# Two-part activations in one pass, 48 gathered tokens, gate tiles on GpSimd, in a two-block transformer kernel

## The chip, the cores and the metric

One core of a Trainium2 chip runs the whole program. The metric is device time in microseconds (us) of one execution; the figures for the kernel before are the median and the spread of three runs. A profiled execution of the same kernel gives the trace.

## The reference, cut to what matters

Two transformer blocks of width 1024 run over 256 tokens. Each has a mixer (attention) and then a feed-forward layer that picks single-neuron experts. The change is in that feed-forward layer alone. In both blocks it is the following computation; the second block has its own weights and half as wide queries.

```
def peer_ffn_2(hn, w_peer_q, sub_keys1, sub_keys2, expert_u, expert_v):
    ...
    s1 = jnp.einsum('thd,hkd->thk', q[:, :, 0], sub_keys1)
    s2 = jnp.einsum('thd,hkd->thk', q[:, :, 1], sub_keys2)
    v1, i1 = lax.top_k(s1, PEER_TOPK)          # 16 of 128 keys, 8 heads
    v2, i2 = lax.top_k(s2, PEER_TOPK)
    ...
    sc, pos = lax.top_k(cand, PEER_TOPK)       # 16 of 256 sums
    eidx = jnp.take_along_axis(cidx, pos, axis=-1)   # expert 128 * i1 + i2
    gates = jax.nn.softmax(sc, axis=-1)
    ...
    act = jax.nn.gelu(jnp.einsum('nkd,nd->nk', expert_u[e], xt), approximate=False)
    return jnp.einsum('nk,nkd->nd', g * act, expert_v[e])
```

There are 16384 experts, so `expert_u` and `expert_v` are 64 MB each in fp32. Each token takes 8 x 16 = 128 of them.

## The kernel before, in words

**Two ways to the same sum.** The feed-forward layer is the method `peer` (L907). For 224 of the 256 tokens (`DENSE`) it is dense: all 16384 activations are computed, multiplied with a matrix of gates that is zero for experts not chosen, and summed with all of `expert_v`. For the last 32 tokens (`GATHERED`) the chosen rows of both tables are fetched by index. The 32 tokens times 128 experts lie as 128 partitions by 32 columns: partition p holds token p mod 32 and a quarter of its experts, so each column j is one indirect DMA of 128 rows of 4 KB from GpSimd's queue (`fetch`, L1201).

**Arithmetic in two parts.** An fp32 number is split into a high part in the format fp32r and a low part, the rest. A product is three matmuls: high by high, high by low, low by high (`mm3`, L350). The tokens are split once into `ht`, a tile with both parts next to each other. Weights stream: SyncE's queue loads units of 128 x 1024 fp32 (512 KB) into four `raw` buffers (L313), ScalarE copies the high part (`hi`, L325), VectorE subtracts to get the low part (`lo`, L334). The high and low tiles have three buffers each, and `unit` keeps two units of parts ahead of the matmuls, in program order.

**Order of the work.** Everything is written out in Python in one program order. After each unit of matmuls `tick` advances every running generator by one step, then runs pieces of the top-k up to a budget (`FILL_U`, 1.2 a tick), then issues the waiting `lo`. Each engine works through its own instructions in that order.

**Stage U.** 128 blocks of 128 experts. `project_t` (L497) makes the activations of one block: for each of eight chunks of the width, three matmuls of 224 columns through `mm3` (L353, L354, L355). Two blocks share a PSUM bank; then `activated` (L1047) applies GELU on ScalarE from PSUM into `ga` (128 x 128 x 224 in SBUF), or, for tokens whose gates are there already, GELU in place in PSUM and a VectorE product with `ga` (L1054). The first 40 or so blocks run beside the top-k, which is on VectorE. Then `group` (L1015) makes the gate matrix for four tokens at a time: two one-hot tiles per token by comparing an `iota` row with the token's index (`o2`, L1027, or on ScalarE at L1022 and L1023 for two of four; `o1`, L1028, times the gate), eight fp16 matmuls (L1034, L1035), and one step of ScalarE or VectorE that writes or multiplies `ga` (L1041, L1043). 56 groups are spread up to block 122.

**The gathered tokens.** `spread_picks` (L1167) copies indices, gates and norm factors of the 32 tokens to the 128 partitions with matmuls and small copies. `gathers` (L1186) then runs 64 jobs through three buffers `gathered`: 32 dot products of fetched rows with the token (VectorE, L1216, one every three ticks), and, once V has begun, 32 scaled sums of rows of the second table (VectorE, L1228, one every two ticks). After each job the next fetch goes to GpSimd's queue.

**Stage V.** 128 blocks again; the eight PSUM banks hold the sums of eight chunks of the width. `add_rows` (L1096) uses two matmuls: the high part of the weights by both token parts next to each other, 448 columns (L1099), and the low part by the high token part, 224 columns, into the second half (L1100). `weigh` (L1092) splits four blocks of `ga` at a time (ScalarE L346, VectorE L347). At the end of the layer the halves are added, turned back with transposes (L1141), the gathered sums are folded from 128 partitions to 32 tokens by a matmul (L1136), and both are added into x (`add_to_x`, L528).

Of the kernel before, what the change touches and what calls it, by code (L numbers as in the profile page):

```python
# [24 lines left out]
GATHERED = 32  # L25
DENSE = 256 - GATHERED
SHARE = 128 // GATHERED
# [9 lines left out]
def _columns():  # L37

    off, table = 0, {}
    for name, n in (("ident", 128), ("norm_mix", 8), ("norm_ffn", 8), ("norm_ple", 8), ("norm1", 8),  # L40
                    ("norm2", 8), ("norm_o", 8), ("b_gate", 2), ("na_q", 1), ("na_k", 1), ("dil_q", 64),
                    ("dil_k", 64), ("cos", 16), ("sin", 16), ("vmask", 8), ("kmask", 32), ("ends", 2), ("repeat", 128),
                    ("fold", GATHERED)):
# [52 lines left out]
def _arrays(a):  # L96
# [104 lines left out]
    put(cst, "repeat", p[:, None] == 128 - GATHERED + p[None, :] % GATHERED)  # L201
    put(cst, "fold", p[:, None] % GATHERED == np.arange(GATHERED)[None, :])
# [30 lines left out]
class Kernel:  # L233
# [269 lines left out]

    def begin_t(self, ht, outs):
# [402 lines left out]
    def peer(self, n, sides_apart, aim, prefetch):  # L907
# [107 lines left out]
        def group(g):  # L1015
            o2 = side.tile([128, 4, 128], F16, tag="o2", name="o2", bufs=2)
            o1 = work.tile([128, 4, 128], F32, tag="row4", name="o1", bufs=2)
            n = self.BY_SCALAR
            if n:
                away = side.tile([128, n, 128], F16, tag="away", name="away", bufs=1)  # L1020
                for j in range(n):
                    nc.scalar.activation(away[:, j], self.iota, AF.Abs, scale=-1.0, bias=i2t[:, 4 * g + j:4 * g + j + 1])  # L1022
                nc.scalar.activation(o2[:, :n], away, AF.Relu, scale=-1.0, bias=1.0)  # L1023
# [23 lines left out]
        def activated(pair, b):  # L1047
            s = slice(2 * pair, 2 * pair + 2)
            t0 = 4 * state["groups"]
            if t0 < DENSE:  # L1050
                self.curve(ga[:, s, t0:], b[:, :, t0:], AF.Gelu)
# [4 lines left out]
            return  # L1056
            yield
# [5 lines left out]
        for blk in range(128):  # L1063
            if blk % 2 == 0:
                b = self.bank().rearrange("p (j t) -> p j t", j=2)[:, :, dense]
            self.project_t(ht, b[:, blk % 2], dense)
            if blk % 2:
# [882 lines left out]
```

## Time and profile before

| | |
|---|---|
| median of three runs | 1943.38 us (1942.16 to 1945.08) |
| the profiled execution | 1939.94 us, span 1938.2 us |
| TensorE matmul busy | 1913.2 us (99%) |
| VectorE busy | 1551.3 us (80%) |
| ScalarE busy | 1131.0 us (58%) |
| GpSimd busy | 181.8 us (9%) |
| moved by DMA | 412.39 MB, mean 213 GB/s |
| first layer: U, then V from | 277.8 us, 654.0 us |
| second layer: U, then V from | 1218.5 us, 1598.3 us |

Engines are named PE (TensorE matmul), PEld (TensorE weight load), DVE (VectorE), ACT (ScalarE), POOL (GpSimd) and SP (SyncE). Times run from the start of the span. Matmuls overlap each other, so the spacing of their starts tells their cost, not their length; a VectorE row is some 0.08 us longer than its spacing too. Durations on POOL are rough.

### The profile page before, as it was taken

How to read it: one execution, taken by the hardware profiler on the slowest of the kernel's cores; microseconds unless marked ns; L12 is line 12 of the kernel's file. 1: busy time of each engine (PE TensorE's matmuls, PEld its weight loads, DVE VectorE, ACT ScalarE, POOL GpSimd, SP SyncE). 2: the span in 40 equal slices, each digit the busy share in tenths (PEclk: the TensorE clock that was granted, in tenths of full speed). 3: DMA queues.
4: the chain of work that ended last, by engine and by line, in shares of the span. 5: the costliest groups of instructions: out<-in, count | busy, mean ns of one | idle time of the engine just before them, and what ended most of it. 6: DMA issues, size and time to landing. Idle time of an engine off the chain costs nothing.

```text
span 1938.2 us, 37562 instructions
## 1 busy us (share of the span) xinstructions
PE 1913.2 (99%) x14666; PEld 1815.0 (94%) x14666; DVE 1551.3 (80%) x3188; ACT 1131.0 (58%) x1833; POOL 181.8 (9%) x142
## 2 busy tenths in 40 slices
PE   8999999999999999999999999999999999999997
PEld 7899999999999999999979979999999999999997
DVE  6865899989999877765577568998899997787655
ACT  5555555577776554445465655555777765545554
POOL 1000000010010223300000000000100012333000
PEclk9999999999999999999999999999999999999999
DMA  7453556667777888776654324566677778888663
GB/s 251 151 159 103 177 164 198 197 220 230 234 230 230 271 292 313 294 241 210 216 168 150 109 63 156 175 204 193 221 225 228 222 229 295 301 313 310 219 226 120
DMA packets 114433, 412.39 MB, mean 213 GB/s; under 512 B 12720, under 2 KB 13888, under 8 KB 114256
## 3 DMA queue, kind: packets, MB, share of 16 engines
q1 hardware_dynamic: 93168, 337.16, 54.1%
q0 software_dynamic: 18432, 67.12, 9.9%
q10 hardware_dynamic: 2656, 5.73, 0.9%
q8 instruction: 115, 1.88, 0.4%
q14 instruction: 62, 0.51, 0.1%
HBM read 408.90 MB, written 1.05 MB: 212 GB/s over the span
## 4 chain that ended last, share of the span: by engine, by line
PE 87%; DVE 9%; ACT 2%; issue 1%; DMA 1%; DVEq 0%; ACTq 0%
PE bank L1099 21%; PE bank L353 16%; PE bank L354 16%; PE bank L355 16%; PE bank L1100 10%; DVE lo L334 4%; DVE o L1028 1%; PE bank L1034 1%; PE bank L1035 1%; PE bank L1775 1%; DVE gathered L1216 1%; DVE ga L1043 1%; PE bank L512 1%; DVE repeated L1228 1%; ACT hi L325 0%
## 5 line engine op out<-in xcount | busy, mean ns | idle before, releaser
L325 ACT ACTIVATE hi<-raw 128x1024 fp32r<-128x1024 f32 x639 | 675.6, 1059 | 692.4 <-PE bank L354 288.0
L334 DVE TENSOR_TENSOR lo<-raw,hi 128x1024 fp32r<-128x1024 f32 x639 | 772.2, 1218 | 104.2 <-ACT hi L325 103.8
L353 PE MATMUL bank<-ht,hi 128*128 128x224 f32 (+1 forms) x2336 | 654.8, 280 | 0.0
L1099 PE MATMUL bank<-ht,hi 128*128 128x448 f32 x2048 | 650.1, 376 | 0.5 <-DVE ht L347 0.5
L355 PE MATMUL bank<-ht,lo 128*128 128x224 f32 (+1 forms) x2336 | 643.2, 275 | 1.2 <-DVE lo L334 1.2
L354 PE MATMUL bank<-ht,hi 128*128 128x224 f32 (+1 forms) x2336 | 642.8, 275 | 0.0
L1100 PE MATMUL bank<-ht,lo 128*128 128x224 f32 x2048 | 544.6, 266 | 1.6 <-DVE lo L334 0.3
L355 PEld LDWEIGHTS bank<-ht,lo 128*128 128x128 f32 x2336 | 447.5, 192 | 1.9 <-DVE lo L334 1.7
L353 PEld LDWEIGHTS bank<-ht,hi 128*128 128x128 f32 x2336 | 447.0, 191 | 1.7 <-ACT hi L325 0.3
L354 PEld LDWEIGHTS bank<-ht,hi 128*128 128x128 f32 x2336 | 447.4, 192 | 0.0
L1099 PEld LDWEIGHTS bank<-ht,hi 128*128 128x128 f32 x2048 | 384.1, 188 | 35.8 <-DVE ht L347 0.9
L1100 PEld LDWEIGHTS bank<-ht,lo 128*128 128x128 f32 x2048 | 391.1, 191 | 7.5 <-DVE lo L334 7.5
L1205 POOL DMA_INDIRECT gathered<-in_rows_dram,index x64 | 69.2, 1082 | 1224.2 <-DVE o L1028 440.6
L347 DVE TENSOR_TENSOR ht<-ga,ht 128x896 fp32r<-128x896 f32 (+2 forms) x78 | 75.6, 979 | 125.5 <-ACT ht L346 125.5
L1028 DVE TENSOR_SCALAR o<-iota,i1t,pack 128x128 f32<-128x128 f16 x448 | 142.6, 340 | 0.0
L1205 POOL DMA_INDIRECT gathered<-in_v_dram,index x64 | 105.0, 1640 | 227.5 <-DVE repeated L1228 191.3
L354 PE MATMUL bank<-lo,ht 128*128 128x512 f32 (+1 forms) x224 | 80.1, 358 | 2.7 <-DVE lo L334 2.7
L353 PE MATMUL bank<-hi,ht 128*128 128x512 f32 (+1 forms) x224 | 81.7, 365 | 0.5 <-ACT hi L325 0.5
L355 PE MATMUL bank<-hi,ht 128*128 128x512 f32 (+1 forms) x224 | 80.0, 357 | 0.6 <-DVE ht L447 0.6
L1228 DVE SCALAR_TENSOR_TENSOR repeated<-gathered,pick_dot,repeated 128x1024 f32<-128x1024 f32 x62 | 79.3, 1279 | 0.0
L1216 DVE CUSTOM_DVE_ANT_0 gathered<-gathered,repeated 128x1024 f32<-128x1024 f32 x64 | 77.7, 1215 | 0.0
L1022 ACT ACTIVATE away<-iota,i2t 128x128 f16<-128x128 f16 x224 | 76.3, 390 | 0.0
(363 smaller groups left out, 2129.8 us busy)
## 6 DMA issues: line engine op xcount, KB each, us to landing
raw<-in_u_dram SPq DMA_DIRECT2D x256, 512.0 KB, 4.2
raw<-in_v_dram SPq DMA_DIRECT2D x256, 512.0 KB, 4.7
raw<-in_w_qkv_dram SPq DMA_DIRECT2D x30, 512.0 KB, 4.3
raw<-in_w_q_dram SPq DMA_DIRECT2D x24, 512.0 KB, 3.5
raw<-in_w_t_dram SPq DMA_DIRECT2D x21, 512.0 KB, 3.6
raw<-in_w_gates_dram SPq DMA_DIRECT2D x16, 512.0 KB, 3.5
raw<-in_w_branch_dram SPq DMA_DIRECT2D x14, 512.0 KB, 3.5
raw<-in_w_pg_dram SPq DMA_DIRECT2D x8, 512.0 KB, 4.3
```

The costliest lines, as they stand in the source:

```text
L325: self.nc.scalar.activation(parts[0], raw, AF.Copy)
L334: self.nc.vector.tensor_tensor(lo, raw, hi.bitcast(F32), op=OP.subtract)
L353: mm(out, l[0], r[0], start=start, stop=False, **kw)
L354: mm(out, l[0], r[1], start=False, stop=False, **kw)
L355: mm(out, l[1], r[0], start=False, stop=stop, **kw)
L1022: nc.scalar.activation(away[:, j], self.iota, AF.Abs, scale=-1.0, bias=i2t[:, 4 * g + j:4 * g + j + 1])
L1028: nc.vector.tensor_scalar(o1[:, j], self.iota, i1t[:, t:t + 1], pf[:, t:t + 1], op0=OP.is_equal, op1=OP.mult)
L1099: mm(acc[c], v[0][:, c], weights[i][:, :, j], start=blk == 0, stop=False, skip_group_check=True)
L1100: mm(acc[c][:, 1], v[1][:, c], weights[i][:, 0, j], start=False, stop=blk == 127, skip_group_check=True)
L1205: nc.gpsimd.indirect_dma_start(out=rows[i], out_offset=None, in_=tables[t], in_offset=bass.IndirectOffsetOnAxis(ap=picks["index"][:, j:j + ...
L1216: nc.vector.tensor_tensor_reduce(r, r, picks["normed"], 1.0, 0.0, OP.mult, OP.add, w[:, j:j + 1])
L1228: nc.vector.scalar_tensor_tensor(total, r, w[:, j:j + 1], total, op0=OP.mult, op1=OP.add)
```

## The change

Five things change, in both layers.

1. U uses two matmuls per chunk as V does (`project_pairs`): the high weights by both token parts, and the low weights by the high part into the second half. A block now has its own PSUM bank; `activated` copies the second half to SBUF on ScalarE, adds the first half on VectorE into a tile `total`, and applies GELU and the gate product there. It runs over several ticks, and V begins only when it is done.
2. 48 tokens are gathered, in sets of 32 and 16 (`SETS`); `DENSE` is 208, and there are 52 groups. The set of 16 has eight partitions per token and 16 columns. There are 96 jobs instead of 64.
3. All gate tiles are made on GpSimd, two ticks ahead of their matmuls instead of one.
4. 14 dots are spread over the last 86 blocks of U; the other 34 and all 48 sums over the first 116 ticks of V. The sums of both sets are interleaved; those of the small set run on GpSimd as a scaling and an addition.
5. Spreading the picks uses a mask and a reduction; folding uses one more bank, two matmuls and one more addition.

The diff, cut (tables of constants and pool declarations left out):

```
-GATHERED = 32
-DENSE = 256 - GATHERED
+SETS = ((32, 96), (16, 80))
+DENSE = 256 - sum(n for n, _ in SETS)
+FOLD = 64
...
+    def project_pairs(self, ht, out, s):
+        w = self.unit(8)
+        mm = self.nc.tensor.matmul
+        for k in range(8):
+            pair = ht[k // 4][:, :, k % 4, s]
+            mm(out, w[0][:, k], pair, start=k == 0, stop=False, skip_group_check=True)
+            mm(out[:, 1], w[1][:, k], pair[:, 0], start=False, stop=k == 7, skip_group_check=True)
+        self.tick()
...
         def group(g):
-            n = self.BY_SCALAR
-            ...
             for j in range(4):
                 t = 4 * g + j
-                if j >= n:
-                    nc.vector.tensor_scalar(o2[:, j], self.iota, i2t[:, t:t + 1], None, op0=OP.is_equal)
-                nc.vector.tensor_scalar(o1[:, j], self.iota, i1t[:, t:t + 1], pf[:, t:t + 1],
+                nc.gpsimd.tensor_scalar(o2[:, j], self.iota, i2t[:, t:t + 1], None, op0=OP.is_equal)
+                nc.gpsimd.tensor_scalar(o1[:, j], self.iota, i1t[:, t:t + 1], pf[:, t:t + 1],
                                         op0=OP.is_equal, op1=OP.mult)
+            yield
             yield
...
-        def activated(pair, b):
+        def activated(pair, banks):
+            total = pool.tile([128, 2, DENSE], F32, tag="total", name="total", bufs=2)
+            yield
+            for j, b in enumerate(banks):
+                nc.scalar.activation(total[:, j], b[:, 1], AF.Copy)
+                nc.vector.tensor_tensor(total[:, j], b[:, 0], total[:, j], op=OP.add)
+                yield
             ...
-                self.curve(b[:, :, :t0], b[:, :, :t0], AF.Gelu)
-                nc.vector.tensor_tensor(ga[:, s, :t0], ga[:, s, :t0], b[:, :, :t0], op=OP.mult)
+                self.curve(total[:, :, :t0], total[:, :, :t0], AF.Gelu)
+                nc.vector.tensor_tensor(ga[:, s, :t0], ga[:, s, :t0], total[:, :, :t0], op=OP.mult)
...
-            self.project_t(ht, b[:, blk % 2], dense)
-            if blk % 2:
-                self.start(activated(blk // 2, b))
+            pair.append(self.bank()[:, :2 * DENSE].rearrange("p (s t) -> p s t", s=2))
+            if blk % 2 == 0:
+                self.start(activated(blk // 2, pair))
+            self.project_pairs(ht, pair[-1], dense)
...
-        while state["groups"] < n_groups:
+        while state["groups"] < n_groups or state["blocks"] < 128:
...
+            for j, name in enumerate(("index", "gate")):
+                part = t[:, j].rearrange("p (g m) -> p g m", m=m)
+                nc.vector.tensor_tensor(part, b[:, 128 * j:128 * (j + 1)].rearrange("p (g m) -> p g m", m=m), own, op=OP.mult)
+                nc.vector.tensor_reduce(t[:, 2 + j, :m], part.rearrange("p g m -> p m g"), AX.X, OP.add)
+                nc.vector.tensor_copy(p[name], t[:, 2 + j, :m])
...
-    EVERY = (3, 2)
+    DOTS, LAST_PICK = 14, 116
...
+        def job(at):
+            t, i, j = jobs[at]
+            r, p = rows.pop(at), picks[i]
+            w, total = p["dot"], p["rows"]
             if t == 0:
-                nc.vector.tensor_tensor_reduce(r, r, picks["normed"], 1.0, 0.0, OP.mult, OP.add, w[:, j:j + 1])
+                nc.vector.tensor_tensor_reduce(r, r, total, 1.0, 0.0, OP.mult, OP.add, w[:, j:j + 1])
+            elif j == 0:
+                nc.vector.tensor_scalar(total, r, w[:, :1], None, op0=OP.mult)
+            elif i == 0:
+                nc.vector.scalar_tensor_tensor(total, r, w[:, j:j + 1], total, op0=OP.mult, op1=OP.add)
             else:
+                nc.gpsimd.tensor_scalar(r, r, w[:, j:j + 1], None, op0=OP.mult)
+                nc.gpsimd.tensor_tensor(total, total, r, op=OP.add)
...
+        while at < len(jobs):
+            yield
+            if rate is None and "second" in self.done:
+                rate, due = (len(jobs) - at) / self.LAST_PICK, 0.0
+            due += rate or self.DOTS / 86
+            while due >= 1.0 and at < len(jobs):
+                due -= 1.0
+                ...
+                job(at)
+                fetch(at + 3)
+                at += 1
```

## Rows read from the trace of the kernel before

**Rows 1.** Busy time by window, with granted clock, DMA share and GB/s.
```profile
core 0: us, PE busy (x) PEld busy (x) DVE busy (x) ACT busy (x) POOL busy (x), PEclk, DMA share, GB/s
278.00:340.00 62.00, 62.00 (x558) 62.00 (x557) 61.93 (x269) 36.88 (x42) 0.00 (x0) 1.00 0.62 192
430.00:590.00 160.00, 160.00 (x1560) 159.13 (x1560) 152.39 (x370) 116.09 (x252) 16.96 (x18) 1.00 0.73 231
690.00:850.00 160.00, 158.83 (x979) 146.25 (x978) 124.82 (x109) 77.89 (x77) 46.97 (x28) 1.00 0.79 293
1650.00:1800.00 150.00, 150.00 (x949) 141.78 (x949) 119.39 (x104) 75.34 (x75) 45.97 (x28) 1.00 0.89 309
```

**Rows 2.** Timeline of PE in U: start us, length us, engine, line, operation.
```profile
603.02 0.28 PE L353 MATMUL bank<-ht,hi 128*128 128x224 f32 x1
...
603.36 0.27 PE L353 MATMUL bank<-ht,hi 128*128 128x224 f32 x1
...
603.70 0.23 PE L1034 MATMUL bank<-o,o 128*128 128x128 f16 x1
...
604.13 0.35 PE L353 MATMUL bank<-ht,hi 128*128 128x224 f32 x1
604.32 0.28 PE L354 MATMUL bank<-ht,hi 128*128 128x224 f32 x1
```

**Rows 3.** Timeline of PE in V, first and last of 16 pairs.
```profile
880.42 0.38 PE L1099 MATMUL bank<-ht,hi 128*128 128x448 f32 x1
...
885.48 0.38 PE L1099 MATMUL bank<-ht,hi 128*128 128x448 f32 x1
```

**Rows 4.** Timeline of DVE during the top-k, two neighbouring splits.
```profile
318.55 1.21 DVE L334 TENSOR_TENSOR lo<-raw,hi 128x1024 fp32r<-128x1024 f32 x1
...
321.11 1.20 DVE L334 TENSOR_TENSOR lo<-raw,hi 128x1024 fp32r<-128x1024 f32 x1
```

**Rows 5.** Groups of DVE instructions: 970 to 990 us, then 430 to 590.
```profile
L1131 DVE TENSOR_TENSOR ga<-bank,ga 128x224 f32<-128x224 f32 x8 | 2.8, 387 | 2.5 <-ACT ga L1130 2.5
...
L334 DVE TENSOR_TENSOR lo<-raw,hi 128x1024 fp32r<-128x1024 f32 x53 | 64.4, 1214 | 0.0
L1028 DVE TENSOR_SCALAR o<-iota,i1t,pack 128x128 f32<-128x128 f16 x146 | 46.9, 344 | 0.0
L1216 DVE CUSTOM_DVE_ANT_0 gathered<-gathered,repeated 128x1024 f32<-128x1024 f32 x18 | 21.9, 1216 | 0.0
L1027 DVE TENSOR_SCALAR o<-iota,i2t 128x128 f16<-128x128 f16 x73 | 18.9, 259 | 0.0
```

**Rows 6.** Timeline of PE: fp32 matmuls of 512 columns, repeating and folding.
```profile
398.15 1.02 PE L1193 MATMUL bank<-x,cst 128*128 128x512 f32 x2
...
981.92 1.04 PE L1136 MATMUL bank<-repeated,cst 128*32 128x512 f32 x2
```

**Rows 7.** Groups of POOL instructions other than DMA: busy us, mean ns.
```profile
L586 POOL MEMSET vdil<- 128x3072 f32 x1 | 2.6, 2648 | 0.0
...
L1735 POOL MEMSET attn<- 128x512 f32 x2 | 1.0, 524 | 0.0
L1887 POOL IOTA iota<- 128x256 f16 x1 | 0.4, 407 | 0.0
L589 POOL MEMSET weights<- 128x128 f32 x2 | 0.3, 194 | 0.0
L1889 POOL IOTA iota<- 128x128 f16 x1 | 0.2, 228 | 0.0
```

**Rows 8.** Timeline of POOL in U, and of DVE and POOL in V.
```profile
479.23 0.94 POOL L1205 DMA_INDIRECT gathered<-in_rows_dram,index  x1 [8.58 <-DVE o L1028]
...
722.67 2.35 DVE L334 TENSOR_TENSOR lo<-raw,hi 128x1024 fp32r<-128x1024 f32 x2
723.03 1.68 POOL L1205 DMA_INDIRECT gathered<-in_v_dram,index  x1 [5.31 <-DVE repeated L1228]
```

**Rows 9.** Groups of DVE instructions in V, 690 to 850 us.
```profile
L1228 DVE SCALAR_TENSOR_TENSOR repeated<-gathered,pick_dot,repeated 128x1024 f32<-128x1024 f32 x31 | 39.6, 1279 | 0.0
L347 DVE TENSOR_TENSOR ht<-ga,ht 128x896 fp32r<-128x896 f32 x16 | 17.5, 1092 | 33.1 <-ACT ht L346 33.1
```

**Rows 10.** DMA issues, median us to landing: 690 to 750, then 1700 to 1800.
```profile
gathered<-in_v_dram,index POOLq DMA_INDIRECT x12, 6.4
...
gathered<-in_v_dram,index POOLq DMA_INDIRECT x19, 8.2
```

More of the change, by code (lines that the diff above doesn't have):

```diff
@@ L530, in add_to_x @@
         end = at + src.shape[1]
-        xs = self.x[:, tt, at:end]
+        xs = self.x[:src.shape[0], tt, at:end]
         self.nc.vector.tensor_tensor(xs, xs, src, op=OP.add)
@@ L1135, in peer @@
                 s = slice(512 * half, 512 * (half + 1))
-                nc.tensor.matmul(banks[1][128 - GATHERED:, :], self.c("fold"), picks["sum"][:, s], start=True, stop=True)
+                folded = self.bank()
+                for i, p in enumerate(picks):
+                    nc.tensor.matmul(folded[FOLD:], self.c(f"fold{i}"), p["rows"][:, s], start=i == 0, stop=i == len(SETS) - 1)
                 for k in range(4):
@@ L1189, in gathers @@
             yield
-        for half in range(2):
-            s = slice(512 * half, 512 * (half + 1))
-            b = self.bank()
-            nc.tensor.matmul(b, self.c("repeat"), self.x[:, 1, s], start=True, stop=True)
-            yield
-            h = picks["normed"][:, s]
-            nc.vector.scalar_tensor_tensor(h, b, picks["y"][:, 1:2], h, op0=OP.mult, op1=OP.mult)
-        tables = (self.d[f"rows{n}"], self.d[f"v{n}"].rearrange("b p d -> (b p) d"))
-        jobs = [(t, j) for t in range(2) for j in range(GATHERED)]
@@ L1199, in gathers @@
-        rows = {}
-        def fetch(i):
-            if i < len(jobs):
-                t, j = jobs[i]
-                rows[i] = pool.tile([128, 1024], F32, tag="gathered", name="gathered", bufs=3)
-                nc.gpsimd.indirect_dma_start(out=rows[i], out_offset=None, in_=tables[t],
-                                             in_offset=bass.IndirectOffsetOnAxis(ap=picks["index"][:, j:j + 1], axis=0))
-        for i in range(3):
-            fetch(i)
-        w = picks["dot"]
-        for i, (t, j) in enumerate(jobs):
-            for _ in range(self.EVERY["second" in self.done]):
-                yield
-            r = rows.pop(i)
-            if t == 0:
-                nc.vector.tensor_tensor_reduce(r, r, picks["normed"], 1.0, 0.0, OP.mult, OP.add, w[:, j:j + 1])
-            else:
-                if j == 0:
-                    while "second" not in self.done:
-                        yield
-                    self.curve(w, w, AF.Gelu)
+        for i, p in enumerate(picks):
+            for half in range(2):
+                s = slice(512 * half, 512 * (half + 1))
+                b = self.bank()
+                nc.tensor.matmul(b, self.c(f"repeat{i}"), self.x[:, 1, s], start=True, stop=True)
+                yield
+                h = p["rows"][:, s]
+                nc.vector.scalar_tensor_tensor(h, b, p["y"], h, op0=OP.mult, op1=OP.mult)
@@ new lines, in gathers, with fetch @@
+        tables = (self.d[f"rows{n}"], self.d[f"v{n}"].rearrange("b p d -> (b p) d"))
+        columns = [(i, j) for i, (m, _) in enumerate(SETS) for j in range(m)]
+        jobs = [(0, *c) for c in columns] + [(1, *c) for c in sorted(columns, key=lambda c: (c[1] + 0.5) / SETS[c[0]][0])]
+        rows = {}
+        def fetch(at):
+            if at < len(jobs):
+                t, i, j = jobs[at]
+                rows[at] = pool.tile([128, 1024], F32, tag="gathered", name="gathered", bufs=3)
+                nc.gpsimd.indirect_dma_start(out=rows[at], out_offset=None, in_=tables[t],
+                                             in_offset=bass.IndirectOffsetOnAxis(ap=picks[i]["index"][:, j:j + 1], axis=0))
@@ new lines, in gathers @@
+        for at in range(3):
+            fetch(at)
+        at, due, rate = 0, 0.0, None
+        while at < len(jobs):
+            yield
+            if rate is None and "second" in self.done:
[3 more added lines that the diff above has]
+                due -= 1.0
+                if at == len(columns):
+                    for p in picks:
+                        self.curve(p["dot"], p["dot"], AF.Gelu)
```

78 lines of the change are left out of this document (39 added, 39 removed).

## The prediction, made blind

> **What bounds the kernel now.** I read the windows table first, then the matmul timeline in two kinds of stage, then VectorE's timeline and groups, then the DMA rows. The profiled execution took 1939.94 us, 1.7 us more than its span of 1938.2. In every window TensorE is busy all or nearly all the time and the granted clock is 1.00, the 2.4 GHz level [rows 1]. So TensorE's own work sets the end, and what counts is the spacing of matmul starts and who becomes late when it shrinks. The change touches two stages, each run twice: U (128 blocks of activations) and V (128 blocks of output sums). In U three 224-column matmuls start in 0.34 us (603.02 to 603.36) [rows 2]; with 0.1114 us each a block of eight such triples takes 2.674 us. The gate group between two blocks (eight fp16 matmuls) adds 0.43 us and stretches the first step behind it from 0.11 to 0.19: 0.51 us. In V, 16 pairs of 448 and 224 columns start in 5.06 us (880.42 to 885.48) [rows 3]: 0.316 us a pair, 2.53 us a block. Both stages stream 672 columns per chunk of weights, yet V is 5% cheaper, because it has two matmuls where U has three.
>
> The same windows show how little room VectorE has in U: 61.93 of 62 us in the first part (where the top-k runs beside the blocks) and 152.39 of 160 in the second (where the gate tiles are made). In V it is at 124.8 of 160 us, and the DMA share is 0.79 in the first V and 0.89 in the second, for 293 and 309 GB/s [rows 1].
>
> **The change part by part, for one of the two layers.**
>
> *Price of the new pair.* U and V both become pairs of 416 and 208 columns. No row has this shape. Low end: all scales with columns, 0.316 x 624/672 = 0.294 us. High end: the short matmul gains nothing, only the 32 columns off the wide one at 2.4 GHz go, 0.316 - 0.013 = 0.303. I take 0.300, nearer the high end, since three 224-column matmuls at 0.1114 show a cost per instruction beyond their 0.093 us of columns. A block is then 2.40 us.
>
> *U, first part* (277.8 to 394 us, 43.5 blocks). VectorE sets the pace: from one `lo` to the next, with six top-k steps between, it needs 2.56 us (318.55 to 321.11) [rows 4], under TensorE's 2.674 but over the new 2.40. The change adds one addition per block here (PSUM plus SBUF, 208 wide; the 224-wide row is 387 ns long [rows 5], about 0.08 of that under the next, so 0.30 us). Some 24 blocks then take 2.86 us and some 19 with bigger top-k steps about 2.60 (estimate: `lo` 1.14, one step near 1.2, the addition 0.3): 118 us where 43.5 x 2.674 = 116 were. The saved matmul is lost here: +3 us with the remainder. Spreading two sets instead of one adds two fp32 repeat matmuls (two took 1.02 us [rows 6]) and three narrow ones: +1.5.
>
> *U, second part* (394 to 653.9 us, 84 blocks). TensorE saves 84 x (2.674 - 2.40) = 23.0 us, and four of 56 groups, 2.0 us. VectorE loses its gate tiles (46.9 + 18.9 us of the 160 in the window [rows 5]) and most dots, and gains the additions; at about three quarters of the time it is no bound. Four ScalarE instructions a group go too, and one copy a block comes. GpSimd takes 52 x 8 = 416 tile operations. No row shows one. Nearest are its IOTA at 128 elements, 0.228 us, and at 256, 0.407 [rows 7]; above I allow two passes, 0.41, below the memset, 0.194. I take 0.27: 112 us of the 230 that TensorE needs. But these operations read SBUF beside VectorE's operations with two SBUF inputs, `lo`, the product with ga (which now reads SBUF instead of PSUM) and the dots: 84 x 1.14 + 42 x 0.3 + 14 x 1.23 = 126 us. If they only alternate, 126 + 112 = 238, so I charge 7 us: -18. Two ticks lie between making and using a tile; if that cover goes, the PE queue stops at the group's first matmul.
>
> That they take turns is what the trace lets one think: an indirect DMA takes GpSimd 0.94 us in U (479.23), but 1.68 when started 0.36 us into a `lo` (723.03, `lo` from 722.67), as if its 0.94 began when that `lo` ended near 723.8 [rows 8]. The Trainium skill says so as a rule (SBUF — State Buffer, Who interferes with whom): a VectorE instruction with two SBUF inputs and a GpSimd instruction that reads SBUF exclude each other for their whole length. Row and rule agree here; applied strictly to all tiles it gives the rival on gate tiles below.
>
> *U to V.* The last activation must now be done before V starts: copy, addition, GELU and product, four operations near 0.5 us with TensorE idle: +2 us.
>
> *V, 126 blocks.* First V took 325 us to the fold at 981.9, second 320.5 (measured from the first V matmul, less the 2.5 us of the last two blocks). TensorE's new price is 126 x 2.40 = 302. But 82 of 96 gather jobs now fall in 116 blocks, 0.707 a block where it was one in two: 1.707 x 0.524 = 0.895 MB per block. Dividing rate by share, the rows give full rates of 293/0.79 = 371 and 309/0.89 = 347 GB/s [rows 1], hence 2.41 or 2.58 us a block. I take 2.50 between. VectorE fits barely: per four blocks 4 x 1.14 + 1.0 for the ht part + 2.83 jobs at about 1.2 = 9.0 of 10.0 us, with ht waiting on ScalarE (33.1 us in 160 now [rows 9]). So 116 x 2.50 + 10 x 2.40 = 314: -11 in the first V and -6.5 in the second.
>
> In the last 68 of those blocks the 16 picks of the small set run on GpSimd, one in three jobs: a scaling and an addition of 1024 elements. By the memset slope (0.83 ns per element) they are 0.9 + 1.8 us, by the IOTA slope (1.4) 1.5 + 2.9 [rows 7]. Then it issues the fetch into the same buffer, and with three buffers and a pattern of period three that buffer serves the next small-set pick. So a cycle of three jobs can't be shorter than these two plus the landing, 6.4 us in the first V, 8.2 in the second [rows 10]: 9.1 and 10.9 us by the low price, against 10.6 at 2.50 us a block. The first fits, the second is 0.3 over; with something for the queue I charge 0.5, 16 times: +8. The fetches of the other set queue on GpSimd behind it, and VectorE's sums and `lo` behind those.
>
> The Trainium skill gives a price for the addition alone (GPSIMD Engine Reference, Performance versus the Vector engine: 4497 ns for 2048 elements). Half of it, 2.25 us as an estimate, lies between my two; the cycle in the second V would be some 0.4 us longer and the sum about 7 us higher. No run yet shows it.
>
> *Tail.* A second fold matmul (0.5 us [rows 6]) and one more addition into x, twice: +2.
>
> Sum: first layer 3 + 1.5 - 18 + 2 - 11 + 2 = -20.5, second 3 + 1.5 - 18 + 2 - 6.5 + 8 + 2 = -8. Together -28.5: 1911.4 against the profiled 1939.94. The median of the runs shown is 3.4 us above that execution, so I predict 1914, and range and rivals are on that footing.
>
> **The rivals.**
>
> *All hidden, about 1869.* GpSimd keeps up everywhere and the DMA engines give 373 GB/s at 2.40 us a block. Then U keeps 25 and V gains 23 and 18: 2 x (3 + 1.5 - 25 + 2 + 2) - 41 = -74. For it: 371 GB/s follows from the first V. Against: the second V's share of 0.89 at 309.
>
> *Gate tiles bind U, about 1973, slower.* Place: GpSimd in U's second part. If a tile operation costs 0.34 us (midway between 0.27 and 0.41) and excludes VectorE's two-input work for its length, 416 x 0.34 + 126 = 267 us instead of 238, 29 more a layer. It decides from 0.31 us on, where 126 + 416p passes the 256 us that the part's blocks and groups take now. For it: the 1.68 us row. Against: the start-up of such an instruction need not hold the SBUF. This is the rule of the Trainium skill above, taken strictly.
>
> *GpSimd picks bind V, about 1965, slower.* Place: the cycle of the small set in V. By the IOTA price 4.4 us plus landing is 10.8 and 12.6 us a cycle, which is 16 x (0.2 + 2.0) = 35 us over 10.6, 27 over my sum; if each of the two operations first waits 0.74 us for a running `lo`, as the DMA did, 16 x 2 x 1.5 = 48 more, 1989 in all. I take the middle of 1941 and 1989. It decides where operations plus landing pass 10.6 us. Against: by the memset price it fits.
>
> **How the numbers follow.** My forecast (1890 to 1935) 0.42, all hidden 0.15, gate tiles 0.18, picks 0.20, the last two's mild forms ending near the old time 0.05. Range 1865 to 1980: about 0.1 outside on each side; the likeliest case alone would be 1890 to 1935. A measurement of this kernel can tell about 0.2% (3.9 us) from no change. Faster: 0.42 + 0.15 = 0.57 less a little for the forecast's upper edge, plus a little from mild forms, 0.57; same 0.07; slower 0.36.
>
> **What would show it.** Right: in U a pair starts every 0.29 to 0.31 us; the first 40 blocks of U show VectorE full and TensorE waiting for `lo`; blocks in V near 2.5 us with a DMA share over 0.9. Wrong: gate matmuls waiting for GpSimd tiles (gate-tile rival); sums waiting for gathered rows, with GpSimd busy most of V's last half (picks); V at 2.4 us a block (all hidden). A pair at 0.316 or more would break the price on which all of it rests.

## The result and the profile after

The changed kernel takes 2309.93 us (median of four runs, 2308.25 to 2312.1) against 1942.77 before: a ratio of 1.189, 95% interval 1.187 to 1.191. It is 367 us slower; 1914 was predicted, with 1980 as the upper end.

The page of the changed kernel, its busy times and its chain of waits by engine and by line:

```profile
PE 1992.5 (86%) x12582; PEld 1861.1 (81%) x12582; DVE 1599.7 (69%) x2858; ACT 1076.1 (47%) x1739; POOL 1193.4 (52%) x1098
...
PE 34%; POOL 29%; DVE 17%; DMA 9%; issue 7%; ACT 4%; ACTq 0%; DVEq 0%; SPq 0%
POOL o L1035 17%; POOL o L1034 12%; PE bank L1112 8%; DVE lo L338 8%; DMA raw<-in_v_dram 6%; PE bank L357 5%; PE bank L358 4%; PE bank L359 4%; PE bank L1113 4%; DMA gathered<-in_v_dram,pick_index 3%; PE bank L514 2%; ACT hi L329 2%; DVE gathered L1244 1%; DVE total L1060 1%; PE bank L515 1%
```

The end was set by TensorE's own work before; now 29% of the chain is on GpSimd, and the two lines of the gate tiles (17% and 12%) make it up. Where the time went, from the first matmul of U to the first of V, and in V from the first wide matmul to the last, in the profiled executions:

| us | first U | first V | second U | second V |
|---|---|---|---|---|
| before | 376.2 | 334.0 | 379.8 | 327.2 |
| predicted | 364.7 | 323 | 368.3 | 328.7 |
| after | 514.6 | 364.0 | 535.5 | 367.5 |

So U lost 294 us of the 370 between the two profiled executions, V 70. The windows of the changed kernel, as [rows 1] (the last two are two parts of V):

```profile
core 0: us, PE busy (x) PEld busy (x) DVE busy (x) ACT busy (x) POOL busy (x), PEclk, DMA share, GB/s
278.00:340.00 62.00, 56.12 (x350) 51.52 (x349) 60.69 (x254) 38.08 (x58) 0.00 (x0) 1.00 0.50 170
430.00:590.00 160.00, 116.95 (x718) 110.21 (x718) 73.49 (x117) 60.56 (x124) 158.18 (x182) 0.86 0.42 138
590.00:770.00 180.00, 133.77 (x824) 126.00 (x824) 89.93 (x135) 66.05 (x143) 178.79 (x207) 0.86 0.39 130
850.00:950.00 100.00, 95.33 (x626) 93.21 (x624) 84.28 (x97) 51.92 (x53) 47.94 (x28) 1.00 0.94 342
970.00:1150.00 180.00, 159.23 (x979) 154.00 (x978) 145.89 (x106) 77.22 (x80) 131.62 (x61) 0.94 0.81 288
```

In U's second part GpSimd is busy 158.18 of 160 us, where it had 16.96. TensorE falls from 160.00 to 116.95 and VectorE from 152.39 to 73.49. The granted clock is 0.86 on the mean there, so some of the stretch was at the lower of its two levels (1.2 and 2.4 GHz); before, with TensorE never idle, it was 1.00. GpSimd's 158.18 of 160 us sets the pace there whatever the clock. The GpSimd groups of the changed kernel (line, operation, count, busy us and mean ns) say why:

```profile
L1035 POOL TENSOR_SCALAR o<-iota,i1t,pack 128x128 f32<-128x128 f16 x416 | 406.4, 977 | 0.3
L1034 POOL TENSOR_SCALAR o<-iota,i2t 128x128 f16<-128x128 f16 x416 | 309.9, 745 | 779.5 <-ACT i2t L1377 394.5 <-DMA raw<-in_u_dram 384.2
...
L1250 POOL TENSOR_SCALAR gathered<-gathered,pick_dot 128x1024 f32<-128x1024 f32 x30 | 96.9, 3229 | 7.0 <-DMA gathered<-in_v_dram,pick_index 6.1
L1251 POOL TENSOR_TENSOR repeated<-repeated,gathered 128x1024 f32<-128x1024 f32 x30 | 76.6, 2553 | 2.5
```

The counts are those of the prediction: 416 tile operations a layer. Their mean is 0.745 and 0.977 us, not 0.27: 208 x (0.745 + 0.977) = 358 us a layer, of the 391 between the first tile (401.5) and V (792.6). The fetches in the same stretch are 19.5 us more on GpSimd (16 of 1.22 us), which the prediction's sum for U did not count. And the 358 are mostly the operations' own length, as a stretch of the GpSimd timeline shows (start us, length us):

```profile
442.63 0.60 POOL L1034 TENSOR_SCALAR o<-iota,i2t 128x128 f16<-128x128 f16 x1
443.23 0.78 POOL L1035 TENSOR_SCALAR o<-iota,i1t,pack 128x128 f32<-128x128 f16 x1
444.00 0.60 POOL L1034 TENSOR_SCALAR o<-iota,i2t 128x128 f16<-128x128 f16 x1
444.59 0.78 POOL L1035 TENSOR_SCALAR o<-iota,i1t,pack 128x128 f32<-128x128 f16 x1
```

Back to back they take 0.60 and 0.78 us; 208 such pairs would be 287 of the 358. The group's first fp16 matmul is where TensorE stands for them (waits of the changed kernel in 430 to 590 us: us in total, times, longest):

```profile
PE bank L1042 <- POOL o L1035: 43.2, 34, 2.9
```

### The profile page after: what moved, and what is told of

Its sections match the earlier page's. It is cut to its first block, busy times and chain, and to the rows that moved or that the text cites. A ratio compares the mean times of both kernels' runs of the same rounds, so it can differ in the third digit from the quotient of the medians.

```text
span 2308.2 us, 34191 instructions
## 1 busy us (share of the span) xinstructions
PE 1992.5 (86%) x12582; PEld 1861.1 (81%) x12582; DVE 1599.7 (69%) x2858; ACT 1076.1 (47%) x1739; POOL 1193.4 (52%) x1098
## 4 chain that ended last, share of the span: by engine, by line
PE 34%; POOL 29%; DVE 17%; DMA 9%; issue 7%; ACT 4%; ACTq 0%; DVEq 0%; SPq 0%
POOL o L1035 17%; POOL o L1034 12%; PE bank L1112 8%; DVE lo L338 8%; DMA raw<-in_v_dram 6%; PE bank L357 5%; PE bank L358 4%; PE bank L359 4%; PE bank L1113 4%; DMA gathered<-in_v_dram,pick_index 3%; PE bank L514 2%; ACT hi L329 2%; DVE gathered L1244 1%; DVE total L1060 1%; PE bank L515 1%
## 5 line engine op out<-in xcount | busy, mean ns | idle before, releaser
L514 PE MATMUL bank<-ht,hi 128*128 128x416 f32 x2048 | 725.2, 409 | 0.0
L1034 POOL TENSOR_SCALAR o<-iota,i2t 128x128 f16<-128x128 f16 x416 | 309.9, 745 | 779.5 <-ACT i2t L1377 394.5
L1112 PE MATMUL bank<-ht,hi 128*128 128x416 f32 x2048 | 645.2, 379 | 6.5 <-DVE ht L351 6.5
L1113 PE MATMUL bank<-ht,lo 128*128 128x208 f32 x2048 | 544.4, 266 | 66.9 <-DVE lo L338 66.8
L515 PE MATMUL bank<-ht,lo 128*128 128x208 f32 x2048 | 573.8, 280 | 26.5 <-DVE lo L338 25.6
L514 PEld LDWEIGHTS bank<-ht,hi 128*128 128x128 f32 x2048 | 433.9, 212 | 8.9 <-issue 0.7
L1112 PEld LDWEIGHTS bank<-ht,hi 128*128 128x128 f32 x2048 | 398.5, 195 | 11.1 <-DVE ht L351 3.6
L1035 POOL TENSOR_SCALAR o<-iota,i1t,pack 128x128 f32<-128x128 f16 x416 | 406.4, 977 | 0.3
L1042 PE MATMUL bank<-o,o 128*128 128x128 f16 x416 | 81.2, 229 | 194.6 <-POOL o L1035 194.1
L1236 POOL DMA_INDIRECT gathered<-in_rows_dram,pick_index x96 | 144.7, 1508 | 171.5 <-DVE pick_dot L1244 161.8
L1236 POOL DMA_INDIRECT gathered<-in_v_dram,pick_index x96 | 159.1, 1657 | 73.9 <-DVE repeated L1248 33.3
L351 DVE TENSOR_TENSOR ht<-ga,ht 128x832 fp32r<-128x832 f32 (+2 forms) x78 | 79.9, 1034 | 70.0 <-ACT ht L350 65.6
L1060 DVE TENSOR_TENSOR total<-bank,total 128x208 f32<-128x208 f32 x256 | 94.1, 367 | 44.4 <-ACT total L1059 43.6
```

The lines of the kernel that those rows point to most:

```text
L514: mm(out, w[0][:, k], pair, start=k == 0, stop=False, skip_group_check=True)
L515: mm(out[:, 1], w[1][:, k], pair[:, 0], start=False, stop=k == 7, skip_group_check=True)
L1034: nc.gpsimd.tensor_scalar(o2[:, j], self.iota, i2t[:, t:t + 1], None, op0=OP.is_equal)
L1035: nc.gpsimd.tensor_scalar(o1[:, j], self.iota, i1t[:, t:t + 1], pf[:, t:t + 1], op0=OP.is_equal, op1=OP.mult)
L1060: nc.vector.tensor_tensor(total[:, j], b[:, 0], total[:, j], op=OP.add)
L1112: mm(acc[c], v[0][:, c], weights[i][:, :, j], start=blk == 0, stop=False, skip_group_check=True)
```

## The experiments

All are timed against the kernel before on the same chip; the ratios have 95% intervals. The first four split the loss.

**One: the gate tiles back on VectorE and ScalarE.**

```diff
 def group(g):  # kernel after
-    nc.gpsimd.tensor_scalar(o2[:, j], ..., op0=OP.is_equal)
-    nc.gpsimd.tensor_scalar(o1[:, j], ..., op0=OP.is_equal, op1=OP.mult)
+    # two o2 by ScalarE's Abs and Relu, two by VectorE, o1 by VectorE
```

> The changed kernel with its gate tiles made as in the kernel before (of each four one-hot tiles two on ScalarE, the rest on VectorE), all else kept. Theory 'tile price' (GpSimd needs 0.745 and 0.977 us per tile operation, 358 us a layer, and TensorE waits for it): VectorE needs about 52 x 1.36 = 71 us for them beside some 173 us of other work in U's second part, so that part falls from about 378 us to 245 to 260, both layers together 235 to 265 us: 2045 to 2075 us. Rival 'cover' (two ticks of lead or two buffers are too few, whichever engine makes the tiles): little changes, 2250 to 2310. Rival 'additions' (the copy and addition of the halves hold U back): no more than 60 us off, above 2250.

Measured 2029.66 us, ratio 1.045 [1.042, 1.049]. 280 of the 367 us go with this edit alone, a little more than the theory's 235 to 265; U is back at 377.6 and 390.9. V is not: 367.5 and 366.2. The two ticks between making and using a tile stay as they are, so the rival "cover" falls.

**Two: the small set's sums on VectorE as one multiply-add.**

```diff
-    nc.gpsimd.tensor_scalar(r, r, w[:, j:j + 1], None, op0=OP.mult)
-    nc.gpsimd.tensor_tensor(total, total, r, op=OP.add)
+    nc.vector.scalar_tensor_tensor(total, r, w[:, j:j + 1], total, op0=OP.mult, op1=OP.add)
```

> The changed kernel with the sums of the small set on VectorE as one multiply-add each instead of two GpSimd operations, all else kept. Theory 'shared port' (GpSimd's scaling and addition of 3.2 and 2.55 us keep VectorE from its two-input work and delay the fetches behind them): V falls from 364 to 325 to 335 us a layer, 2230 to 2255 us in all. Rival 'DMA' (V is held by 0.895 MB per block): V stays above 350 us, 2285 to 2310.

2272.12, ratio 1.169 [1.167, 1.171]: 38 us, between the two expectations. In its profiled execution (2286.08 us, the longest of the five) V falls to 355 and 349, not to 330, so the GpSimd picks are only part of V's loss.

**Three: both edits** (the two diffs above together).

> Both edits together: GpSimd computes nothing, only issues fetches. Theory (GpSimd's compute is the whole loss): the losses add, 1960 to 2000 us, within 3% of the kernel before; U's first part still some 8 us longer a layer, V near 320 to 330. If below 1935, the pairs and the 48 tokens pay once GpSimd is free. Rival 'DMA' in V: above 2030.

1991.11, ratio 1.027 [1.024, 1.030]. The two add up (280 + 38 = 318; measured 319), so neither hid the other. 48 us stay: what is left of the change is itself slower than before. V is at 348 and 350, where 320 to 330 had been expected.

**Four: the kernel before, with only its gate tiles on GpSimd.**

```diff
 def group(g):  # kernel before
-    # two o2 by ScalarE's Abs and Relu, two by VectorE, o1 by VectorE
+    nc.gpsimd.tensor_scalar(o2[:, j], ..., op0=OP.is_equal)
+    nc.gpsimd.tensor_scalar(o1[:, j], ..., op0=OP.is_equal, op1=OP.mult)
+    yield   # used two ticks later
```

> The kernel before with one edit: all gate tiles made on GpSimd, two ticks ahead. Theory 'tile price': 56 groups x 8 operations at 0.86 us are 386 us a layer for a part that took 260 us, plus fetches: 2180 to 2240 us. Without waits at the port (0.60 and 0.78 us as their shortest) 309 us a layer: about 2045 to 2070. Rival 'cover' or 'additions' (the loss needs the new activations): 1935 to 1960.

2319.79, ratio 1.195 [1.193, 1.196], above what was expected and even above the whole change: the one move is enough for the whole loss. Its 448 + 448 operations:

```profile
L1021 POOL TENSOR_SCALAR o<-iota,i1t,pack 128x128 f32<-128x128 f16 x448 | 487.0, 1087 | 0.0
L1020 POOL TENSOR_SCALAR o<-iota,i2t 128x128 f16<-128x128 f16 x448 | 303.3, 677 | 752.6 <-ACT i2t L1328 750.5
```

There are 32 more a layer than in the changed kernel, and the pair of them is 1.76 us instead of 1.72. And 30 and 27 fetches, of 1.14 and 1.11 us on GpSimd, stand among the tiles of the two layers, where the changed kernel has 16 and 14.

**Five: the operations alone and side by side.** A program without matmuls runs 24 tile operations, then six scalings and six additions of 1024 elements, alone, beside VectorE's subtraction of two SBUF tiles, and beside an addition that reads PSUM; one kind of tile also beside VectorE's own fp16 comparisons.

```diff
+gate2 = lambda k: P.tensor_scalar(o2[:, k % 4], self.iota, ids[...], None, op0=OP.is_equal)
+lo = lambda k: V.tensor_tensor(big["lo"], big["raw"], big["hi"], op=OP.subtract)
+psum = lambda k: V.tensor_tensor(big["total"][:, :512], bank, big["total"][:, :512], op=OP.add)
+for ops in ([(gate2, 24)], [(gate1, 24)], ..., [(gate2, 24), (lo, 12)], ..., [(gate2, 24), (psum, 24)], ...):
```

> None of the reference is computed here: GpSimd's and VectorE's operations run by themselves and side by side, with nothing that waits for a matrix product. Theory (each GpSimd tile operation has a length of its own far above the 0.27 us of the prediction, and VectorE's two-input operations lengthen it further): alone 0.58 to 0.62 us with one operation and 0.76 to 0.80 us with two; beside VectorE's subtraction of two tiles in SBUF a mean of 0.75 to 1.3 us; beside a VectorE operation with one input in PSUM about as alone; scaling 1024 columns alone 1.6 to 3.0 us and adding 2.0 to 2.6 us, each longer by at least a quarter beside the subtraction. Rival (the lengths in the kernel are waits of the tiles' buffers put down to the operations): alone 0.25 to 0.45 us, and within 10% of that beside any VectorE operation.

Its timeline (a row is a run of operations and its length that of the whole run, the count at its end). Alone (GpSimd's four kinds, then VectorE's subtraction):

```profile
9.86 13.96 POOL L1958 TENSOR_SCALAR o<-iota,ids 128x128 f16<-128x128 f16 x24
...
24.39 18.64 POOL L1959 TENSOR_SCALAR o<-iota,ids 128x128 f32<-128x128 f16 x24
...
43.58 17.54 POOL L1960 TENSOR_SCALAR port_a<-port_a,ids 128x1024 f32<-128x1024 f32 x6
...
61.66 14.43 POOL L1961 TENSOR_TENSOR port_b<-port_b,port_a 128x1024 f32<-128x1024 f32 x6
...
76.32 10.04 DVE L1962 TENSOR_TENSOR port_lo<-port_raw,port_hi 128x1024 fp32r<-128x1024 f32 x8
```

That is 0.58, 0.78, 2.92 and 2.41 us each, and 1.26 for the subtraction. The theory on lengths holds and the rival, 0.25 to 0.45, falls: they are GpSimd's own. Side by side, in stretches in which both engines ran (VectorE runs the subtraction at first, the addition from PSUM at 185.78, the comparisons at 203.14, and the subtraction again at 250.24):

```profile
110.77 15.35 POOL L1958 TENSOR_SCALAR o<-iota,ids 128x128 f16<-128x128 f16 x12
```
```profile
134.56 18.53 POOL L1959 TENSOR_SCALAR o<-iota,ids 128x128 f32<-128x128 f16 x13
```
```profile
109.53 15.54 DVE L1962 TENSOR_TENSOR port_lo<-port_raw,port_hi 128x1024 fp32r<-128x1024 f32 x12
...
185.78 13.94 POOL L1958 TENSOR_SCALAR o<-iota,ids 128x128 f16<-128x128 f16 x24
```
```profile
203.14 20.57 POOL L1959 TENSOR_SCALAR o<-iota,ids 128x128 f32<-128x128 f16 x20
```
```profile
250.24 16.50 DVE L1962 TENSOR_TENSOR port_lo<-port_raw,port_hi 128x1024 fp32r<-128x1024 f32 x5
```
```profile
250.22 18.73 POOL L1961 TENSOR_TENSOR port_b<-port_b,port_a 128x1024 f32<-128x1024 f32 x6
```

Beside the subtraction a tile takes 1.28 us instead of 0.58 (15.35 / 12) and 1.43 instead of 0.78 (18.53 / 13, above the 1.3 expected): about one subtraction goes by for each tile, and the subtraction itself barely notices (15.54 / 12 = 1.30). Beside VectorE reading PSUM a tile takes 0.58, as alone. Beside VectorE's fp16 comparisons, which have one SBUF input, the two-operation tile takes 1.03 instead of 0.78 (20.57 / 20), which the theory did not have. With the long GpSimd addition both pay: a subtraction takes 3.30 us instead of 1.26 (16.50 / 5), the addition 3.12 instead of 2.41 (18.73 / 6). The scaling, 3.41 us beside the subtraction, grew by 17%, less than the quarter expected.

**Six: only o2 on GpSimd**, with the picks on VectorE as in two.

```diff
-    nc.gpsimd.tensor_scalar(o1[:, j], ..., op0=OP.is_equal, op1=OP.mult)
+    nc.vector.tensor_scalar(o1[:, j], ..., op0=OP.is_equal, op1=OP.mult)
```

> The changed kernel with all sums on VectorE and only the one-operation tiles (o2) on GpSimd; the two-operation tiles (o1) are on VectorE. Theory 'tile price': 208 x 0.73 = 152 us a layer on GpSimd fit into the 245 us of U's second part, so TensorE no longer waits for tiles; VectorE loses 17 us and ScalarE 90 us against the version with tiles back: 1970 to 1990 us. Rival 'port' (each GpSimd tile also holds VectorE up, whoever has room): 2000 to 2060.

1994.64, ratio 1.026 [1.023, 1.029]: the same as with no tile there (1991.11), and just above the theory's 1970 to 1990. The window of U and the group of tiles:

```profile
430.00:590.00 160.00, 157.54 (x1198) 150.90 (x1197) 155.09 (x338) 97.39 (x206) 155.19 (x153) 1.00 0.69 221
```
```profile
L1034 POOL TENSOR_SCALAR o<-iota,i2t 128x128 f16<-128x128 f16 x416 | 400.4, 978 | 799.6 <-ACT i2t L1374 778.0 <-PE bank L1043 20.8
```

GpSimd is busy 155.19 of 160 us in U, but TensorE keeps its pace (157.54 of 160 busy). Half the tiles is what it can carry, at no gain. The same tile takes 0.978 us here and 0.745 in the changed kernel: VectorE is busy 155.09 of 160 us beside it, where it was 73.49. So the price of a GpSimd operation depends on what VectorE does beside it, as experiment five has it for one pair of operations at a time.

**Seven: without the one-pass activations** (both moves undone and U's three matmuls back, GELU from PSUM, 208 tokens dense).

```diff
-    self.project_pairs(ht, pair[-1], dense)   # two matmuls, summed outside
+    self.project_t(ht, b[:, blk % 2], dense)  # three matmuls
```

> Tiles and sums off GpSimd, and U as in the kernel before (three matmuls per chunk, now 208 columns, GELU from PSUM, no additions); 48 tokens gathered, dots mostly later. Theory 'VectorE sets U' (the additions cost what the matmuls save): U falls from 378 and 391 us to 355 to 375, 1945 to 1970 us in all. Rival 'pairs pay' (TensorE sets U): 2000 to 2050, since 24 matmuls at 0.111 us are 0.27 us a block more than 8 pairs at 0.300.

1975.36, ratio 1.017 [1.015, 1.019], a little above the theory's 1945 to 1970 (U takes 376.3 and 377.7 us, not 355 to 375): the pairs, which save TensorE 0.03 us of 0.33 a chunk, cost 16 us. The windows of U's first and second part, first with both moves undone, then with the three matmuls too:

```profile
278.00:340.00 62.00, 56.23 (x351) 51.71 (x350) 60.69 (x253) 38.02 (x59) 0.00 (x0) 1.00 0.51 170
430.00:590.00 160.00, 157.36 (x1199) 150.84 (x1198) 159.07 (x408) 131.83 (x314) 10.29 (x9) 1.00 0.65 210
```
```profile
278.00:340.00 62.00, 62.00 (x558) 62.00 (x556) 61.93 (x270) 36.94 (x42) 0.00 (x0) 1.00 0.66 190
...
430.00:590.00 160.00, 160.00 (x1551) 159.42 (x1550) 139.19 (x334) 113.02 (x242) 9.36 (x9) 1.00 0.64 201
```

With the pairs VectorE holds both parts (60.69 of 62, 159.07 of 160) and TensorE has gaps. The first part ends, with the first gate tile, at 405.9 us with pairs and at 395.0 with three matmuls: 11 us lost, since each block brings VectorE an addition. The rest of the first U takes 250 against 259.5 us, so the pairs win 9 of them back; in the second layer they lose 13 in the first part and win nothing. With three matmuls TensorE is full, yet gets nothing for the 16 tokens that it no longer has. Its timeline:

```profile
602.86 0.27 PE L357 MATMUL bank<-ht,hi 128*128 128x208 f32 x1
...
603.86 0.28 PE L357 MATMUL bank<-ht,hi 128*128 128x208 f32 x1
```

Nine matmuls of 208 columns start in 1.00 us, three in 0.33; three of 224 started in 0.34 [rows 2]. Weight loads are busy 159.42 of 160 us in that window.

**Eight and nine: what holds V?** With both moves undone, once without the fetches of the second table, once with sums over 8 of 1024 columns.

```diff
-rows[at] = pool.tile([128, 1024], F32, tag="gathered", ...)   # eight: a fixed tile, no DMA for t == 1
-nc.vector.scalar_tensor_tensor(total, r, ...)                  # nine: [:, :8] of total and r
```

> Tiles and sums off GpSimd; left out are the fetches of rows of the second table (the sums run on whatever rows lie in the three buffers). Theory 'DMA' (V is held by bytes): V falls from 348 and 350 us to 318 to 328, 1935 to 1950 us. Rival 'VectorE' (V is held by the dots and sums): within 10 us of 1991.

> Tiles and sums off GpSimd, all fetches kept; left out are the sums but for 8 of 1024 columns. Theory 'DMA': V stays above 338 us, 1970 to 1991 us. Rival 'VectorE' (48 x 1.2 = 58 us less for it in each V): 1930 to 1950.

1962.23, ratio 1.010 [1.007, 1.014], and 1966.82, 1.013 [1.011, 1.015]: 29 and 24 us faster than with both (1991.11). Neither expected theory is right alone; each load taken away gives part of V back (333 and 331 us without fetches, 334 and 330 without sums). Windows of 800 to 980 us, with both loads, without fetches, without sums:

```profile
800.00:980.00 180.00, 163.27 (x1055) 158.74 (x1054) 149.06 (x131) 83.83 (x85) 82.74 (x43) 0.99 0.88 324
```
```profile
800.00:980.00 180.00, 176.51 (x1161) 173.10 (x1160) 157.32 (x138) 91.24 (x93) 0.00 (x0) 1.00 0.67 215
```
```profile
800.00:980.00 180.00, 174.76 (x1142) 172.86 (x1141) 111.27 (x138) 89.97 (x90) 56.18 (x43) 0.98 0.92 340
```

At 16 matmuls a block that is 2.73, 2.48 and 2.52 us a block. Without fetches TensorE is busy 176.51 of 180 us, so V is near TensorE's own 2.40 and VectorE, at 157.32, does not hold it by itself. Without sums V moves 340 GB/s at a DMA share of 0.92. With both it takes 2.73, 0.2 more than with either. One could think that the fetches, which GpSimd issues, make VectorE's operations longer. The `lo` of 800 to 960 us, first with fetches and then without, has the same length:

```profile
L338 DVE TENSOR_TENSOR lo<-raw,hi 128x1024 fp32r<-128x1024 f32 x59 | 70.9, 1219 | 0.5 <-ACT hi L329 0.5
```
```profile
L338 DVE TENSOR_TENSOR lo<-raw,hi 128x1024 fp32r<-128x1024 f32 x64 | 76.9, 1217 | 0.0
```

So what V loses are waits, and the granted clock adds to them. With both moves undone TensorE waits for a `lo`, and then its pairs start every 0.56 us, at the lower level, before they are back at 0.30:

```profile
847.20 0.36 PE L1119 MATMUL bank<-ht,lo 128*128 128x208 f32 x1 [2.70 <-DVE lo L338]
...
848.33 0.59 PE L1118 MATMUL bank<-ht,hi 128*128 128x416 f32 x1
...
848.89 0.59 PE L1118 MATMUL bank<-ht,hi 128*128 128x416 f32 x1
...
851.08 0.36 PE L1118 MATMUL bank<-ht,hi 128*128 128x416 f32 x1
...
851.38 0.37 PE L1118 MATMUL bank<-ht,hi 128*128 128x416 f32 x1
```

The mean granted clock of the two V is 1.00 and 1.00 before, 0.96 and 0.95 in the changed kernel, 0.99 and 0.98 with both moves undone. With a mean of c over T us, 2(1 - c)T us are at the lower level, and at most 0.46 of them are lost, since 0.30 us of work take 0.56. That is at most some 30 us of the changed kernel's two V and some 10 with both moves undone (estimates from these rounded clocks). The clock did not fall with every wait: in U's first part, with TensorE busy 56.12 of 62 us, it was 1.00.

**Ten to twelve: fewer jobs left for V.** From experiment seven, with more of the 48 dot products in U.

```diff
-    DOTS, LAST_PICK = 14, 116
+    DOTS, LAST_PICK = 30, 116     # ten; eleven: 40; twelve: 40 and BY_SCALAR = 4, was 2
```

> The kernel with the old three matmuls and both moves to GpSimd undone (1975), with 30 of the 48 dot products in the second part of U instead of 14, so V has 66 jobs instead of 82. Theory (V is held by its transfers and VectorE together, and U's second part has room on VectorE, 139 of 160 us busy there): V falls from 348 and 338 us to 328 to 336 a layer, U rises by 0 to 4 us a layer, 1945 to 1965 us. Rival (16 more dots of 1.2 us fill the second part of U, so what V gives U takes): 1970 to 1985 us.

> As the kernel with 30 early dot products, with 40: V has 56 jobs. Theory: V at 318 to 330 us a layer, near what TensorE needs for 208 columns, U longer by 4 to 14 us a layer as VectorE fills there; 1925 to 1955 us. Rival (U is full): 1970 to 1995 us, slower than with 30.

1949.43, ratio 1.002 [1.000, 1.004], and 1944.31, ratio 1.000 [0.999, 1.001]: V falls from 348.4 and 337.8 to 331.8 and 332, then to 327.1 and 332.7; the second U rises from 377.7 to 378.7 and 382.4. The theories' times hold; with 40 dots the first V is inside the expected 318 to 330, the second above it. So "dots mostly later" cost 31 us. In the second U with 40, VectorE is at 169.88 of 170 us, which the last one tests by making all `o2` on ScalarE:

> The kernel with 40 early dot products, with all four o2 tiles of a group made on ScalarE instead of two. Theory (in U's second part VectorE is the limit, 169.88 of 170 us busy in the second layer; 104 comparisons of 0.24 us a layer leave it, and ScalarE, 118 of 170 us, takes 104 of 0.39 us): U 4 to 10 us shorter a layer, 1925 to 1938 us, faster than the kernel before. Rival (U's second part goes at TensorE's pace of weight loads, PEld 159.4 of 160 us in the first layer, and VectorE only looks full): 1940 to 1950 us. Third (ScalarE fills, and the split's hi part comes late): over 1950 us.

1939.47, ratio 0.998 [0.997, 0.999] over twelve runs: faster than the kernel before by 0.24%, with an interval that just leaves out 1, and 1.5 us above the range of its theory. Windows of its second U, with 40 dots first:

```profile
1420.00:1590.00 170.00, 167.78 (x1614) 165.16 (x1613) 169.88 (x405) 117.88 (x265) 26.89 (x25) 1.00 0.76 243
```
```profile
1420.00:1590.00 170.00, 170.00 (x1645) 169.14 (x1644) 162.56 (x329) 145.06 (x338) 26.51 (x26) 1.00 0.80 256
```

VectorE gets 7 us of room, U 5 (377.5), and then weight loads are full again (169.14 of 170), as the rival had it. Its profiled execution was the shortest of the twelve (1926 us), so the 5 us are of that execution. Its two V are shorter too (320.5 and 322.8), with a granted clock of 1.00 where 40 dots alone had 0.98.

## Why the prediction was wrong

**The failed step: "I take 0.27", in U's second part.** A tile operation measured 0.745 and 0.977 us in the kernel, 0.58 and 0.78 alone. Even the upper bound, 0.41, was too low by a factor of 1.4 and 1.9. The bounds came from IOTA and MEMSET [rows 7], the only GpSimd rows other than DMA, and these read no tensor. They share the engine with the new operation, not the work; no row bounded it from above, and a bound called "two passes" was made up from a row of another kind. A layer has 416 of them, so each 0.1 us of error was 42 us a layer. With 0.27 the tiles were to take 112 us of 230; they took 358.

**The gate-tile rival had the place and the mechanism, and the wrong size.** GpSimd binds U and TensorE stands at the group's first matmul, as it said; whether it decides from 0.31 us on was not tested. It said 1973, since its price was 0.34. With the lengths alone its own sum, 126 + 208 x (0.58 + 0.78) = 409 us, comes near the 391 measured, in part by luck: VectorE lengthened the tiles by 75 us (358 less 283), not by 126, and some 20 us of fetches were not in the sum. Experiment four shows that this alone makes the loss.

**Turns for the SBUF: right in kind, too strict in length.** Experiment five has it by itself: 1.28 against 0.58 us beside a VectorE operation on two SBUF inputs, 0.58 beside one that reads PSUM. The Trainium skill's rule (SBUF — State Buffer, Who interferes with whom), that a VectorE instruction with two SBUF inputs contends with a GpSimd instruction that reads SBUF, agrees with these numbers. That each shuts the other out for its whole length, as the prediction put it, does not come out: a subtraction and a tile would need 1.26 + 0.58 = 1.84 us and take 1.30, a subtraction and an addition 3.67 and take 3.30. So some 0.4 to 0.5 us of each GpSimd operation passes beside VectorE, which fits the prediction's own point against the rival; which part of the operation that is was not measured. Who pays depends on the length of the GpSimd operation: VectorE's subtraction takes 1.30 us beside a tile and 3.30 beside the addition.

**The pick rival came true too.** It took 1.5 + 2.9 us by the IOTA slope; measured 3.23 + 2.55 in the kernel, 2.92 + 2.41 alone. The addition was bounded well, the scaling was twice its high price. Moving the picks back won 38 us, 30 more than the 8 charged, near the low end of the rival's 27 to 75 over the forecast. The two rivals had been weighed as alternatives, and both happened; the range reached to either, never to their sum. Even their sum, 1914 + 59 + 51 = 2024, would have been far below 2310, so the price of a tile is what failed. The delays are plain in the timeline of the first V, where a GpSimd addition lies on a `lo` (1.21 us without it [rows 4]) and on a sum (1.28 [rows 9]):

```profile
1008.49 2.71 POOL L1251 TENSOR_TENSOR repeated<-repeated,gathered 128x1024 f32<-128x1024 f32 x1
...
1008.87 3.42 DVE L338 TENSOR_TENSOR lo<-raw,hi 128x1024 fp32r<-128x1024 f32 x1
...
1020.70 2.38 POOL L1251 TENSOR_TENSOR repeated<-repeated,gathered 128x1024 f32<-128x1024 f32 x1
1020.72 3.43 DVE L1248 SCALAR_TENSOR_TENSOR repeated<-gathered,pick_dot,repeated 128x1024 f32<-128x1024 f32 x1 [2.91 <-DMA gathered<-in_v_dram,pick_index]
```

The Trainium skill's price (GPSIMD Engine Reference, Performance versus the Vector engine), halved, was an estimate of 2.25 us for the addition; the run has 2.41.

**V at 2.50 us a block: wrong.** It took the transfers' 2.41 to 2.58 and let VectorE's 9.0 of 10.0 us pass beside them. Without sums V takes 2.52 us a block, without fetches 2.48, with both 2.73: the missing term is what the two loads cost each other in waits, 0.2 us a block. The prediction also kept the granted clock at 1.00, and in V it was 0.96 and 0.95. The full DMA rate was right (340 / 0.92 = 370 and 342 / 0.94 = 364 GB/s, where 347 to 371 were taken).

**Right.** The price of the pair, 0.300 us (PE timeline of the first V of the changed kernel):

```profile
1099.84 0.36 PE L1112 MATMUL bank<-ht,hi 128*128 128x416 f32 x1
...
1100.14 0.36 PE L1112 MATMUL bank<-ht,hi 128*128 128x416 f32 x1
```

U's first part, in kind: VectorE full (60.69 of 62), TensorE waiting for `lo`, a loss where TensorE saves; but the tiles begin at 401.5 instead of 394.8, and at 405.9 with them back on VectorE, so +7 to +11 where +4.5 was the sum. U to V: TensorE idle for 3.4 us where +2 was charged.

**Without the moves.** VectorE, which the prediction had "no bound" at three quarters in U's second part once its tiles are gone, is the bound as soon as they come back (159.07 of 160). So the pairs needed the room that moving the tiles was to make, and GpSimd could not take the tiles.

**The sum of the causes**, by medians, from after back to before: tiles 280 and picks 38 (319 together), pairs 16, dots moved late 31; 1944.31 is left, the time before. These steps were taken in this order, and another order could divide the loss otherwise. What remains of the change at its best, 16 tokens less for TensorE, came to 4.7 us, with `o2` moved to ScalarE; whether that move alone would help the kernel before was not tried. Why the two loads in V cost each other waits, by the three buffers between them or in some other way, was not separated; nor was the clock's part.

## What to carry to other kernels

Before work is moved to an engine, price it by a row of the same kind of operation on that engine; where there is none, an IOTA or a MEMSET is no upper bound, and a count of 416 makes the unknown price the whole answer, so the range has to reach as far as the ignorance does. Test the move by "at what length does it bind" (0.31 us here, by the prediction's estimate) and treat that as the forecast's hinge. Price it beside its neighbours too: a tile of 0.58 us alone took 0.745 and 0.978 in two kernels. Where two resources are each near 90% of a stage's time, leave room for their waits: in V the two together were slower than either, while in U before TensorE and VectorE ran at 62.00 and 61.93 of 62 us without a loss [rows 1].

## What the runs showed that was not expected

- A GpSimd comparison of 128 x 128 fp16 takes 0.58 us, with a second operation and fp32 output 0.78; VectorE's rows of the same two were 0.259 and 0.344 [rows 5].
- Scaling 1024 columns by a column of numbers, with one tensor input, is slower on GpSimd (2.92 us) than adding two tensors (2.41).
- Three fp32r matmuls a chunk keep a spacing of 0.111 us at 208 columns as at 224: in this form fewer columns gained TensorE nothing.
- After a wait of 2.70 us in V TensorE's pairs went on at 0.56 us for a while, at the lower clock level, instead of 0.30: here the clock added to the waits.
